# First layer's experts in order of load, 128 slots for six and 64 for ten, plain float32 products on unsplit weights

## The chip, the cores and the metric

The kernel runs on one core of a Trainium2 chip. The metric is the device time of one execution in microseconds (us), the median of several runs. All numbers here are of that core.

## The reference, cut to what matters

The reference is a two-layer hybrid diffusion backbone on 512 tokens (256 of a context, 256 of the image) of width 1024. Each layer has token mixers and then a mixture of 16 experts, of which each token takes two. Layer 0 computes its experts for all 512 tokens, layer 1 for the last 256. What the change touches is this:

```python
def _moe(h, router_w, router_b, w_gate, w_up, w_down):
    scores = jax.nn.sigmoid(h.astype(F32) @ router_w.astype(F32))
    ...
    _, idx = lax.top_k(jnp.where(in_grp, sel, -jnp.inf), TOP_K)
    ...
    combine = jnp.sum(jax.nn.one_hot(idx, N_EXPERTS, dtype=F32) * w[..., None], axis=1)
    out = jnp.zeros(h.shape, F32)
    for e in range(N_EXPERTS):
        act = jax.nn.silu(h @ w_gate[e]) * (h @ w_up[e])
        out = out + combine[:, e:e + 1] * (act @ w_down[e])
    return out.astype(h.dtype)
```

An expert's gate and up weights are 1024 x 512 each, its down weights 512 x 1024, all float32: six chunks of 1 MB.

## The kernel before, in words

A scheduler orders each engine's instructions when the kernel is built: tiles come from pools with a fixed number of buffers under a tag (`TILES`, `BANKS`), and the program's text sets priorities. Weights come through a ring of six 1 MB tiles, three under each of two tags (`RINGS`, `load`, L2064), in the order of use, issued on SP's queue.

Layer 0 (`moe`, L1780). `route` (L1600) scores the tokens on TensorE and VectorE (DVE), finds each token's two experts and its rank among an expert's tokens, by a running count on TensorE (L1659 to L1661, into `ps_route`), and the largest count, `rt_mxi`. `token_rows` (L1696) turns the normalised tokens to rows and keeps each as a high and a low part of type float32r (float32 words that TensorE multiplies at reduced precision). `gather` (L1809 on) builds a 0/1 selection `sel` of tokens against 128 slots for two experts at once (L1811), and multiplies it with the high and the low rows apart: 64 products of 256 columns (L1820) for a pair of experts. Copies to `xe` follow on DVE (L1826) and ScalarE (ACT, L1824).

Each expert then has 128 slots. Its weights are split into a high part by ACT (L152) and a low part by DVE (L153), 1024 columns at a time, and each product is made of three float32r products of 512 columns (L1804 to L1806): high x high, high x low, low x high. That makes 48 for gate and up and 24 for down. Between them stand the activation (L1862, L1863), the transposes of the activations (L1869, `ps_actT`) and their split (L1871, L1872). The result `y` of experts 0 to 14 is written to DRAM (L1894, on ACT's queue). Behind expert 14, GpSimd (POOL) fetches two rows of it for every token by eight indirect DMAs (L1904); ACT and DVE weight and add them (L1906, L1907). Expert 15 goes back to the tokens by products (L1914), and products with the identity (L1918) add the fetched rows in PSUM; DVE adds the result to the residual (`xT`, L1925). Three pieces of layer 1's conditioning (`between`, L1301, weights `in_w_ada`) run beside this end.

`overflow` (L1714) stands behind the first gather: each engine loads `rt_mxi` (L1734) and branches (L1735) around a loop over all experts that runs only where an expert has more tokens than slots.

Layer 1 (`moe_small`, L1929) already has 64 slots and plain float32 products on the weights as they come. The gate and up products of 256 columns run on the two 64-column halves of the array at a time (L1996), so do the down products of 512 (L2026). Its loads are the same ring.

## Time and profile before

| | |
|---|---|
| median of 3 runs | 1566.8 us (1566.14 to 1569.63) |
| profiled execution | 1576.39 us |
| its span, first to last instruction | 1574.6 us |
| mean granted TensorE clock | 0.929 |
| PE, DVE, ACT, POOL busy | 88%, 60%, 38%, 24% |
| DMA moved | 337.68 MB, 214 GB/s over the span |
| layer 0's experts, first product to the last y in DRAM | 533 to 861 us |
| its end, to the last residual | 861 to 900 us |
| layer 1's experts | 1312 to 1558 us |

PE is TensorE multiplying, PEld TensorE loading the operand that stays in the array, SP the engine that issues the loads of weights; PEq, SPq and so on are the engines' sequencers. A granted clock of 1.00 is TensorE's upper level, 2.4 GHz. A stretch is read by its own row, since stages of the program have different limits. Busy times of the profile are sums of instructions' durations; TensorE's instructions overlap, so what a run of products costs is read from the distance of their starts.

### The profile page before, as it was taken

To read this page: it belongs to the slowest core of one execution; us is meant where nothing else is said; L and a number is where in the kernel's file an instruction comes from. 1 tells how busy PE (TensorE), PEld (TensorE's weight loads), DVE (VectorE), ACT (ScalarE), POOL (GpSimd) and SP (SyncE) were. 2 spreads that over 40 slices of the span, in tenths; PEclk is the share of its full clock that TensorE was granted. 3 is DMA by queue.
4 is the path that set the end of the run, shared out by engine and by line. 5 is a ranking of instruction groups with operands and counts; after the bars stand their busy time and mean duration, and the time that the engine had idled before them with its cause. 6 is when DMAs were issued, how large, how long until landed. Compare 5 with 4: busy or idle time off the path is not lost. (4 is left out here: it accounts for less than half of the span.)

```text
span 1574.6 us, 28837 instructions
## 1 busy us (share of the span) xinstructions
PE 1390.1 (88%) x11950; PEld 1077.8 (68%) x11950; DVE 949.7 (60%) x1534; ACT 605.4 (38%) x908; POOL 372.1 (24%) x425
## 2 busy tenths in 40 slices
PE   5697869998998799999999877895999987999996
PEld 1596559888774688888887567675877765554553
DVE  5795793558444787879798669588345653111112
ACT  3353213433423576767677343421334350000001
POOL 1645252336101000000000665534133410000000
PEclk9797888999999899999999989796879998999999
DMA  9231334133426586969798712053325735999995
GB/s 380 68 99 46 96 138 136 63 108 122 176 80 263 199 338 268 366 269 368 267 383 334 311 32 98 30 171 130 122 80 198 274 133 212 389 393 401 405 418 214
DMA packets 83730, 337.68 MB, mean 214 GB/s; under 512 B 32278, under 2 KB 37208, under 8 KB 48904
## 3 DMA queue, kind: packets, MB, share of 16 engines
q1 hardware_dynamic: 79784, 320.36, 53.9%
q10 hardware_dynamic: 2160, 7.87, 1.2%
q0 software_dynamic: 1648, 7.54, 1.2%
q8 instruction: 97, 1.59, 0.4%
q14 instruction: 41, 0.34, 0.1%
HBM read 312.95 MB, written 22.77 MB: 213 GB/s over the span
## 5 line engine op out<-in xcount | busy, mean ns | idle before, releaser
L153 DVE TENSOR_TENSOR w_lo<-ring,w_hi 128x1024 fp32r<-128x1024 f32 x192 | 226.4, 1219 | 24.6 <-ACT w_hi L152 22.7
L152 ACT ACTIVATE w_hi<-ring 128x1024 fp32r<-128x1024 f32 x192 | 198.3, 1059 | 53.5 <-PE ps_up L1805 31.7
L1380 PE MATMUL ps_project<-h_hi,wi_lo 128*128 128x256 f32 (+1 forms) x568 | 138.3, 309 | 26.2 <-DVE wi_lo L153 26.1
L1380 PE MATMUL ps_project<-h_hi,wi_hi 128*128 128x256 f32 (+1 forms) x568 | 136.7, 308 | 13.8 <-ACT h_hi L1368 8.3
L1380 PE MATMUL ps_project<-h_lo,wi_hi 128*128 128x256 f32 (+1 forms) x568 | 134.1, 302 | 5.2 <-DVE h_lo L1369 5.2
L1996 PE MATMUL ps_up<-ring,xe 128*64 128x256 f32 x1024 | 120.8, 382 | 7.4 <-DMA ring<-in_w_moe 5.2
L1380 PEld LDWEIGHTS ps_project<-h_hi,wi_lo 128*128 128x128 f32 (+1 forms) x568 | 98.2, 203 | 34.5 <-DVE wi_lo L153 29.4
L1380 PEld LDWEIGHTS ps_project<-h_hi,wi_hi 128*128 128x128 f32 (+1 forms) x568 | 97.9, 203 | 18.7 <-ACT h_hi L1368 8.4
L1996 PEld LDWEIGHTS ps_up<-ring,xe 128*64 128x64 f32 x1024 | 72.0, 137 | 53.1 <-issue 14.9
L1805 PE MATMUL ps_up<-w_lo,xe 128*128 128x512 f32 x256 | 101.6, 397 | 4.9 <-DVE w_lo L153 4.3
L1380 PEld LDWEIGHTS ps_project<-h_lo,wi_hi 128*128 128x128 f32 (+1 forms) x568 | 97.5, 201 | 8.6 <-DVE h_lo L1369 5.7
L1804 PE MATMUL ps_up<-w_hi,xe 128*128 128x512 f32 x256 | 100.2, 394 | 1.9 <-PEq L1735 1.9
L1806 PE MATMUL ps_up<-w_hi,xe 128*128 128x512 f32 x256 | 100.0, 391 | 0.0
L2064 POOL DMA_DIRECT2D ring<-in_w_in x4 | 2.4, 609 | 384.7 <-PE ps_mods L1301 376.4
L153 DVE TENSOR_TENSOR wi_lo<-ring,wi_hi 128x1024 fp32r<-128x1024 f32 (+1 forms) x50 | 69.5, 1396 | 28.3 <-ACT wi_hi L152 20.8
L152 ACT ACTIVATE wi_hi<-ring 128x1024 fp32r<-128x1024 f32 (+1 forms) x50 | 51.2, 1032 | 88.4 <-DMA ring<-in_w_in 43.9
L2008 ACT ACTIVATE act<-ps_up 128x256 f32<-128x256 f32 x16 | 6.1, 383 | 160.4 <-PE ps_up L1996 133.2
L2029 DVE COPY y<-ps_down 128x512 f32<-128x512 f32 x16 | 11.1, 692 | 88.4 <-PE ps_down L2026 88.4
L2026 PE MATMUL ps_down<-ring,actT 128*64 128x512 f32 x256 | 58.6, 596 | 4.5 <-ACT actT L2017 4.5
L1805 PEld LDWEIGHTS ps_up<-w_lo,xe 128*128 128x128 f32 x256 | 48.1, 188 | 17.7 <-DVE w_lo L153 9.0
L1804 PEld LDWEIGHTS ps_up<-w_hi,xe 128*128 128x128 f32 x256 | 48.1, 188 | 12.0 <-ACT xe L1824 2.1
L1806 PEld LDWEIGHTS ps_up<-w_hi,xe 128*128 128x128 f32 x256 | 48.1, 188 | 9.1
(559 smaller groups left out, 3279.8 us busy)
## 6 DMA issues: line engine op xcount, KB each, us to landing
ring<-in_w_moe SPq DMA_DIRECT2D x192, 1024.0 KB
ring<-in_w_ada SPq DMA_DIRECT2D x46, 1024.0 KB
ring<-in_w_in SPq DMA_DIRECT2D x21, 1024.0 KB
ring<-in_w_out SPq DMA_DIRECT2D x8, 1024.0 KB
Y<-y ACTq DMA_DIRECT2D x15, 512.0 KB
xT<-in_xT SPq DMA_DIRECT2D x8, 512.0 KB
ring<-in_w_in POOLq DMA_DIRECT2D x3, 1024.0 KB
w_ada<-in_w_ada SPq DMA_DIRECT2D x4, 512.0 KB
```

The lines of the kernel that those rows point to most:

```text
L152: self.nc.scalar.activation(out[0], src, AF.Copy)
L153: self.nc.vector.tensor_tensor(out[1], src, out[0].bitcast(F32), ALU.subtract)
L1380: nc.tensor.matmul(p[:, c], x[a], w[b][:, c], start=i + a + b + o == 0, stop=i == n - 1 and a == 1, skip_group_check=True)
L1804: nc.tensor.matmul(p, xh, wh, start=first and i == 0, stop=False)
L1805: nc.tensor.matmul(p, xh, wl, start=False, stop=False)
L1806: nc.tensor.matmul(p, xl, wh, start=False, stop=last and i == n - 1)
L1996: nc.tensor.matmul(p[64 * c:64 * c + 64, 128 * j:128 * j + 256], x[4 * half + i], w[:, 512 * i + 256 * c:512 * i + 256 * c + 256], start=h ...
L2008: nc.scalar.activation(act, pu[:, :256], AF.Silu)
L2026: nc.tensor.matmul(p[64 * half:64 * half + 64], aT[:, f * 128 + 64 * c:f * 128 + 64 * c + 64], ds[half][:, 512 * i:512 * i + 512], start=i ...
L2029: nc.vector.tensor_copy(y, p)
L2064: queue.dma_start(w[:, :n], src)
```

## The change

Layer 0 gets a class `Experts` that layer 1 (now `moe_last`) uses as well. `route` with `by_load` sorts the experts on DVE: the counts are ranked by comparing each with each (L1695 to L1697), expert 0 always first; `rt_order` says which expert stands at which place, `rby` holds the ranks by place, and each place gets its first row in Y. The first six places (`BIG`) have 128 slots, the other ten 64; `rt_mxi` is now the largest number of tokens over a place's slots, and `overflow` runs if it is above zero. Places are taken in the order 0, 6, 1, 7, 8, 2, 9, 10, 3, 11, 12, 4, 13, 14, 5, 15, so that two small ones stand between big ones.

The gather adds high and low rows into one float32 `xe`: for place 0 alone 64 products of 128 columns, then five times 64 of 256 columns for a big and two small places. Nothing is split any more. A big place has 16 plain float32 products of 512 columns for gate and up and 8 for down; a small one has 32 of 256 columns and 8 of 512, two at a time on the halves of the array. The loads of all places but the first take the expert's number from a register of SP, which is read from `rt_order` (L1961). A small place's `y` has two writes to Y. The last place goes back to the tokens by eight plain float32 products. Layer 1's arithmetic stays as it was; its `route` leaves out what it did not use.

```diff
-CAPS = (128, 64)
+BIG, CAP_BIG, CAP = 6, 128, 64
...
+ROWS = CAP * VIA + (CAP_BIG - CAP) * BIG
+GROUPS = [(0,)] + [(BIG + 2 * i, i + 1, BIG + 2 * i + 1) for i in range(BIG - 1)]
...
+    v.scalar_tensor_tensor(key, cnt, 16.0, C["first16"], op0=ALU.mult, op1=ALU.add)
+    v.tensor_tensor(sq, key[:, None].to_broadcast([128, 16, 16]), key[:, :, None].to_broadcast([128, 16, 16]), ALU.is_gt)
+    v.tensor_reduce(place, sq, op=ALU.add, axis=AX.X)
...
+    v.tensor_copy(order, key)
+    v.tensor_tensor(big, rsel[:, :, None].to_broadcast([128, nt, 16, 16]), perm[:, None].to_broadcast([128, nt, 16, 16]),
+                    ALU.mult)
+    v.tensor_reduce(rby, big, op=ALU.add, axis=AX.X)
...
-    with k.tc.If(n > cap):
+    with k.tc.If(n > 0):
...
+                for j, rows in enumerate(hi + lo):
+                    nc.tensor.matmul(p[:, i * n:(i + 1) * n], rows[:, ms], sel[j % nt], start=j == 0, stop=j == 2 * nt - 1)
...
+                    if cap == 64:
+                        for c in range(2):
+                            nc.tensor.matmul(out[j][64 * c:64 * c + 64], x(4 * half + i),
+                                             w[:, 512 * i + 256 * c:512 * i + 256 * c + 256], **kw)
+                    else:
+                        nc.tensor.matmul(out[j], x(4 * half + i), w[:, 512 * i:512 * i + 512], **kw)
...
-        qs = [k.parts(w[:, 1024 * i:1024 * i + 1024], "w") for i in range(2)]
...
-            nc.tensor.matmul(p, xh, wh, start=first and i == 0, stop=False)
-            nc.tensor.matmul(p, xh, wl, start=False, stop=False)
-            nc.tensor.matmul(p, xl, wh, start=False, stop=last and i == n - 1)
...
+    first = [load(I["w_moe"][0, i], which=i % 2) for i in range(6)]
+    todo = gather(GROUPS[0])
+    overflow(k, I, h2, xT, mod, cwo, mxi, nt, 0)
+    _, at = nc.values_load_multi_w_load_instructions(order[:1, 1:], engines=(mybir.EngineType.SP,), min_val=0, max_val=15)
+    def weight(r, i):
+        if not r:
+            return first[i]
+        return load(I["w_moe"][bass.ds(at[r - 1], 1), i].rearrange("a p n -> p (a n)"), which=i % 2)
...
+        r, cap, _, sel = todo.pop(0)
+        aT = X.between(*pu, cap)
+        if len(todo) < 2 and groups:
+            todo += gather(groups.pop(0))
+        ds = [weight(r, 4 + half) for half in range(2)]
+        if todo:
+            pu = X.inward(todo[0][2], todo[0][1], lambda i: weight(todo[0][0], i))
+        y = X.outward(aT, cap, ds)
```

The order of the instructions moves at three places.

On PE, the end of the first gather and what follows. Before (`rt_mxi` and the branch behind it are the overflow test):

```order
L1820 MATMUL ps_gather<-sel,h_lo 128x256 x4
L1820 MATMUL ps_gather<-sel,h_hi 128x256 x4
L1820 MATMUL ps_gather<-sel,h_lo 128x256 x4
L1734 TENSOR_LOAD rt_mxi
L1735 COMPARE_AND_BRANCH
L1741 COMPARE_AND_BRANCH
```

The same place with the change:

```order
L1840 MATMUL ps_gather<-sel,h_hi 128x128 x4
L1840 MATMUL ps_gather<-sel,h_lo 128x128 x4
L1866 MATMUL ps_up<-ring,xe 128x512 x16
L1777 TENSOR_LOAD rt_mxi
L1778 COMPARE_AND_BRANCH
L1784 COMPARE_AND_BRANCH
```

The gather has half the columns, and the first expert's 16 gate and up products now stand ahead of the branch. Further on, PE's order for a round of one big and two small places, with the change, is this (128x512 down rows are the big place's, 64x512 the small ones'):

```order
L1863 MATMUL ps_up<-ring,xe 64x256 x16
L1901 MATMUL ps_down<-ring,actT 128x512 x8
L1863 MATMUL ps_up<-ring,xe 64x256 x8
L1878 MATMUL ps_actT<-consts_75,act 128x128 x2
L1863 MATMUL ps_up<-ring,xe 64x256 x16
L1894 MATMUL ps_down<-ring,actT 64x512 x5
L1863 MATMUL ps_up<-ring,xe 64x256 x8
L1894 MATMUL ps_down<-ring,actT 64x512 x3
```

Down products of one place lie between the up products of the next.

On SP, the loads behind the overflow loop. Before, the end of the loop and what follows:

```order
L1741 REGISTER_ALU
L1741 COMPARE_AND_BRANCH
L1741 UNCONDITIONAL_BRANCH
L1735 UNCONDITIONAL_BRANCH x2
L2064 DMA ring<-in_w_moe 128x2048 x90
L2064 DMA ring<-in_w_ada 128x2048 x6
```

With the change, ahead of the branch:

```order
L2090 DMA ring<-in_w_ada 128x2048 x10
L2090 DMA ring<-in_w_moe 128x2048 x6
L1961 TENSOR_LOAD rt_order
L1961 ISA x28
L1777 TENSOR_LOAD rt_mxi
L1777 ISA x2
L1961 ISA x2
L1778 COMPARE_AND_BRANCH
```

and behind the loop:

```order
L1784 UNCONDITIONAL_BRANCH
L1778 UNCONDITIONAL_BRANCH x2
L2090 ISA
L2090 DMA ring<-in_w_moe 128x2048
L2090 ISA
L2090 DMA ring<-in_w_moe 128x2048
```

The order's registers are filled ahead of the branch (ISA rows are register operations), and each load behind it has one register operation of its own.

On DVE, behind the running count in `ps_route`. Before:

```order
L1662 TENSOR_TENSOR rt_rsel<-rt,ps_route 128x64
L1665 TENSOR_REDUCE rt_mx<-ps_route 128x1
L1667 TENSOR_SCALAR rt<-ps_route 128x64
L1811 TENSOR_TENSOR sel<-consts_76,rt_rsel 128x1024
L1666 CAST rt_mxi<-rt_mx 128x1
```

With the change:

```order
L1668 TENSOR_TENSOR rt<-rt,ps_route 128x64
L1695 SCALAR_TENSOR_TENSOR rt_l<-ps_route,consts_76 128x16
L1675 TENSOR_TENSOR rt<-rt 128x64
L1696 TENSOR_TENSOR rt_big<-rt_l 128x256
L1927 TENSOR_TENSOR sel<-consts_76,rt 128x512
L1676 TENSOR_REDUCE rt_s<-rt 128x4
L1697 TENSOR_REDUCE rt_l<-rt_big 128x16
L1675 TENSOR_TENSOR rt<-rt 128x64
L1698 TENSOR_TENSOR rt_l<-rt_l,consts_76 128x256
```

The first selection stands one place later and has half the columns; most of the sort stands behind it, 21 rows of `route` ahead of the first copy of `xe` on DVE and 22 more ahead of the second.

## Rows read from the trace of the kernel before

**Rows 1.** Busy time of an engine: us, share of the span, instructions.

```profile
PE 1390.1 (88%) x11950; PEld 1077.8 (68%) x11950; DVE 949.7 (60%) x1534; ACT 605.4 (38%) x908; POOL 372.1 (24%) x425
```

**Rows 2.** Stretches: length, busy us and count by engine, granted clock, DMA share, GB/s.

```profile
522.00:533.35 11.35, 9.35 (x65) 9.17 (x65) 7.16 (x33) 4.64 (x7) 0.00 (x0) 0.85 0.01 4
533.35:860.50 327.15, 320.91 (x1632) 269.63 (x1633) 275.32 (x273) 234.26 (x267) 0.00 (x0) 1.00 0.84 323
860.50:899.70 39.20, 33.59 (x200) 23.71 (x198) 22.79 (x32) 12.97 (x15) 21.94 (x16) 0.96 0.78 309
...
1311.70:1558.35 246.65, 229.85 (x1689) 132.22 (x1688) 36.11 (x76) 18.90 (x41) 0.00 (x0) 1.00 0.95 384
1350.00:1550.00 200.00, 188.47 (x1378) 106.07 (x1376) 29.46 (x60) 12.24 (x30) 0.00 (x0) 1.00 1.00 403
1390.40:1400.10 9.70, 8.42 (x69) 4.92 (x63) 2.21 (x5) 0.38 (x1) 0.00 (x0) 1.00 1.02 421
```

**Rows 3.** Timeline of PE, fp32r products of an expert: start, us, what.

```profile
542.16 0.39 PE L1806 MATMUL ps_up<-w_hi,xe 128*128 128x512 f32 x1
...
543.07 0.39 PE L1804 MATMUL ps_up<-w_hi,xe 128*128 128x512 f32 x1
```

**Rows 4.** Costliest groups: busy us, mean ns, idle time before and its releaser.

```profile
L153 DVE TENSOR_TENSOR w_lo<-ring,w_hi 128x1024 fp32r<-128x1024 f32 x192 | 226.4, 1219 | 24.6 <-ACT w_hi L152 22.7
```

**Rows 5.** Timeline of PE, first gather, branch and first product.

```profile
522.13 1.23 PE L1820 MATMUL ps_gather<-sel,h_hi 128*128 128x256 f32 x4 [1.66 <-DVE rt_mxi L1666]
...
525.56 0.64 PE L1820 MATMUL ps_gather<-sel,h_hi 128*128 128x256 f32 x4
...
530.83 0.64 PE L1820 MATMUL ps_gather<-sel,h_lo 128*128 128x256 f32 x4
533.35 0.47 PE L1804 MATMUL ps_up<-w_hi,xe 128*128 128x512 f32 x1 [1.88 <-PEq L1735]
```

**Rows 6.** Chain that ended last, layer 1's experts: start, us, what.

```profile
1372.94 3.43 PE ps_down L2026 x16
1376.37 3.45 PE ps_up L1996 x32
...
1390.45 9.61 DMA ring<-in_w_moe
...
1408.04 0.38 PE ps_actT L2015 x2
...
1475.73 5.98 DMA ring<-in_w_moe
```

**Rows 7.** Group, line and timeline of plain float32 products and transposes.

```profile
L2026 PE MATMUL ps_down<-ring,actT 128*64 128x512 f32 x256 | 58.6, 596 | 4.5 <-ACT actT L2017 4.5
L1326 PE MATMUL ps_rstd<-rs,consts x10: 379/592/697, 17.5 to 1565.9; 128*128 128x512 f32 x6, 128*128 128x256 f32 x4
608.38 0.49 PE L1869 MATMUL ps_actT<-consts,act 128*128 128x128 f32 x3
896.35 2.05 PE L1918 MATMUL ps_last<-consts,ya 128*128 128x128 f32 x16 [0.29 <-DVE ya L1907]
```

**Rows 8.** Timeline of DVE, `route` and the first gather.

```profile
520.50 0.22 DVE L1662 TENSOR_TENSOR rt_rsel<-rt,ps_route 128x64 f32<-128x64 f32 x1 [2.41 <-PE ps_route L1661]
520.86 1.22 DVE L1811 TENSOR_TENSOR sel<-consts,rt_rsel 128x1024 fp32r<-128x1024 f32 x1
524.24 0.69 DVE L1826 CAST xe<-ps_gather 128x512 fp32r<-128x512 f32 x1 [0.43 <-PE ps_gather L1820]
```

**Rows 9.** Lines L1734, L2064 on SP's sequencer: ns least/median/most, first and last start.

```profile
L1734 SPq FUSED_REGOPS  x2: 175/181/187, 522.7 to 1307.8; - x2
L2064 SPq DMA_DIRECT2D ring<-in_w_moe x192: 327/328/1358, 490.1 to 1544.1; - x192
```

**Rows 10.** DMA queue of the loads, 1350 to 1550 us: packets, MB, share of 16 engines.

```profile
q1 hardware_dynamic: 11046, 80.46, 99.3%
```

**Rows 11.** Timeline of DVE and POOL behind the 15th expert; indirect DMAs, us to landing.

```profile
859.87 0.69 DVE L1888 COPY y<-ps_down 128x512 f32<-128x512 f32 x1 [0.17 <-PE ps_down L1806]
869.17 1.03 POOL L1904 DMA_INDIRECT ya<-Y,rt_slot  x1 [0.93 <-issue]
877.99 1.16 POOL L1904 DMA_INDIRECT yb<-Y,rt_slot  x1 [0.30 <-issue]
yb<-Y,rt_slot POOLq DMA_INDIRECT x4, 8.9
```

More of the change, by code (lines that the diff above doesn't have):

```diff
@@ L1711, in token_rows, with overflow @@
     return hi, lo
-def overflow(k, I, h2, xT, mod, cwo, mxi, nt, cap, layer):
+def overflow(k, I, h2, xT, mod, cwo, mxi, nt, layer):
     nc, C = k.nc, k.C
@@ L1841, in gather @@
-        return out
-    def into(xs, e, j):
-        p = k.bank("up", "p")[:cap]
-        for half in range(2):
-            product(p, xs[4 * half:4 * half + 4], split(weight(e, j + half)), half == 0, half == 1)
-        return p
-    def weight(e, i):
-        return load_e(e, i) if e else first[i]
-    Y = S["Y"][layer]
-    back, before, ys = [], [], []
-    xs, after = gather(0)
-    first = [load_e(0, i) for i in range(6)]
-    overflow(k, I, h2, xT, mod, cwo, mxi, nt, cap, layer)
-    pg = into(xs, 0, 0)
@@ new lines, in outward @@
+    def outward(self, aT, cap, ds):
+        k, nc = self.k, self.nc
+        y = k.u("y", 8 * cap)
+        if cap == 64:
+            p = k.bank("down", self.acts[2])
+            for i in range(4):
+                for half in range(2):
+                    nc.tensor.matmul(p[64 * half:64 * half + 64], aT[i], ds[half][:, 512 * i:512 * i + 512], start=i == 0,
+                                     stop=i == 3)
+            nc.vector.tensor_copy(y, p)
+        else:
+            for half in range(2):
+                p = k.bank("down", self.acts[2])
+                for i in range(4):
+                    nc.tensor.matmul(p, aT[i], ds[half][:, 512 * i:512 * i + 512], start=i == 0, stop=i == 3)
+                o = y[:, 512 * half:512 * half + 512]
+                if half:
+                    nc.vector.tensor_copy(o, p)
+                else:
+                    nc.scalar.activation(o, p, AF.Copy)
+        return y
@@ L1908, in moe @@
                 before.append(ya)
-    ps = [k.bank("last", "aaaabbpp"[m])[:, :nt * 128] for m in range(8)]
-    for m, p in enumerate(ps):
-        for i in range(16 - VIA):
-            for n, (u, w) in enumerate(((0, 0), (0, 1), (1, 0))):
-                nc.tensor.matmul(p, ys[i][u][:, m * 128:(m + 1) * 128], back[i][:, w], start=i == 0 and n == 0, stop=False,
-                                 skip_group_check=True)
+    ps = [k.bank("last", "aaaabbpp"[m]) for m in range(8)]
+    for m in range(4):
+        for half in range(2):
+            hs = slice(64 * half, 64 * half + 64)
+            nc.tensor.matmul(ps[4 * half + m], y[hs, m * 128:(m + 1) * 128], back[hs], start=True, stop=False,
+                             skip_group_check=True)
     for t in range(nt):
@@ L1982, in moe_small @@
-    xs, sel = gather(0)
+        sel = k.u("sel", nt * 4 * CAP).bitcast(F32R).rearrange("p (t g s) -> p t g s", t=nt, g=4)
+        selection(k, sel, rsel[:, :, e:e + 4], CAP)
+        x = X.gather([sel[:, t].rearrange("p g s -> p (g s)") for t in range(nt)], 4 * CAP, hi, lo)
+        return [(lambda i, a=g * CAP: x(i, a, a + CAP), sel[:, :, g]) for g in range(4)]
+    todo = gather(0)
     first = [load_e(0, i) for i in range(6)]
-    overflow(k, I, h2, xT, mod, cwo, mxi, nt, cap, layer)
+    overflow(k, I, h2, xT, mod, cwo, mxi, nt, 1)
@@ L2030, in moe_small @@
+        _, sel = todo.pop(0)
+        aT = X.between(*pu, CAP)
+        b = X.back(sel, cw[:, :, e])
+        if len(todo) == 2 and e < 12:
+            todo += gather(e + 3)
+        ds = [weight(e, 4 + half) for half in range(2)]
+        if todo:
+            pu = X.inward(todo[0][0], CAP, lambda i: weight(e + 1, i))
+        y = X.outward(aT, CAP, ds)
         for m in range(4):
@@ L2034, in moe_small @@
                                  skip_group_check=True)
-        if e % 4 == 3:
-            xs, sel = after, asel
     k.exp_ln()
```

343 lines of the change are left out of this document (157 added, 186 removed).

## The prediction

> **What bounds the kernel now.** I read the busy shares first: PE is busy 88% of the span [rows 1], so time comes mostly out of TensorE's work. Then the table of stretches [rows 2]. The one that the change rewrites, 533.35 to 860.50 us, has PE busy 320.91 of 327.15 us at granted clock 1.00, the 2.4 GHz level, with DMA at 0.84: TensorE bounds it, and its idle time is 6.2 us. The second layer's expert stretch shows what comes next if TensorE gets less to do: there DMA stands at 0.95 to 1.00 and moves 403 GB/s. The order of work says who waits for whom in between; the timeline and the chain give prices.
>
> The sum is made against the profiled execution (1576.39 us, span 1574.6, so 1.8 us outside). It is 9.6 us above the median 1566.8; I take the difference as a constant and apply the gain to the median. A change of under 0.2% (3 us) could not be told from none.
>
> **What is removed.** Layer 0 makes 72 fp32r products of 512 columns an expert, one each 0.227 us (four steps from 542.16 to 543.07 [rows 3]), 16.3 us an expert. The splits behind them, 192 of 1.22 us on DVE [rows 4] and as many on ACT, go too; they lie beside PE's work, which waited little for them, so I count nothing for them but the 6.2 us that I leave in place as idle time. Seven later gathers of 64 matmuls go; five remain.
>
> **What stands there now,** from the start of the first gather at 522.13 us [rows 5] to the last down product of the 15th expert, after which DVE copies y at 859.87 [rows 11]; all after that hangs on this y.
>
> 1. Plain float32. The trace shows each such product as two records: 256 records for layer 1's 128 down products [rows 7]. Of those, 16 records (8 products, two at a time on the halves of the array) take 3.43 us [rows 6]: 0.86 us for a 512-column pair. A full-width product is a record of the same 592 ns at its median (L1326 [rows 7]), up to 697; I take 0.86 us, the upper end 0.86 x 697/592 = 1.01. A big expert has 24: 20.6 us, six make 124. (Per big expert that is dearer than the 16.3 us now; the gain comes from the small ones.)
> 2. A small expert: 32 records of up products take 3.45 us [rows 6], half of an expert's, so 6.9 us, and its down products 3.43. In the row of 15 experts there are nine small, and by the order a quarter of the 16th's up products stands ahead: 9.25 x 6.9 = 64 and 9 x 3.43 = 31.
> 3. Five gathers of 256 columns: sixteen groups of four at 0.479 us (eleven steps from 525.56 to 530.83 [rows 5]) are 7.7 us each: 38.
> 4. First gather, 64 fp32r matmuls of 128 columns, a shape that the trace lacks. Below: half of the 256-column one, 0.06 us, 3.8 in all. Above: a plain float32 one of 128 columns, 2.05/8 = 0.256 us (L1918 [rows 7]), 16.4 in all. Nearest is the row of the same shape, at clock 0.96; I take 0.2 us, 13.
> 5. Transposes: three in 0.49 us for big ones, two in 0.38 [rows 6, 7]: 6 x 0.65 + 9 x 0.38 = 7. The branch: 1.9 us idle as now [rows 5].
>
> These make 279 us. To them come:
>
> 6. Idle time between groups as now: 6.2.
> 7. The sort. DVE gets some 20 small operations, four of 256 columns (0.2 to 1.2 us each) and two of 1024 (1.22) ahead of the copies of x [rows 8]: about 8 us, beside a first gather of 13. The selection for expert 0 is ahead of nearly all of it, and is half as large as now. The second copy of x may come late: 0 to 5 us, I take 2. Order and register values reach SP by one load and 28 register operations of 0.18 us [rows 9], 5.5 us, done before the first ring slot is free; each later load costs 0.18 on top of 0.33, well within 2.6.
> 8. The ring. 80.46 MB in 200 us [rows 10] is 2.61 us a 1 MB load. Two small experts in a row need 12 loads (31 us) in about 21 us of PE; six lie in the ring. The first slot is free 1.7 us after the first small one starts. The shortest wait for a load in the chain is 5.98 us [rows 6], at most 3.4 more than its 2.61; so the fourth load behind that slot lands by 1.7 + 3.4 + 10.4 = 15.5, just when it is needed, and the last by 20.8, needed at 17.2 or later: 0 to 3.5 us in each of five rounds, 0 to 17 in all. I take 5, since by the order the next expert's up products mostly stand ahead of the last two loads' down products. A whole round has 20.6 + 2 x 10.3 + 7.7 + 1.4 = 50 us of PE against 18 loads, 47 us.
>
> Sum 292 us, so the copy of y starts at 814.3 in place of 859.87: **45.6 us sooner**. The tail from there [rows 2, 11] (Y to DRAM, eight indirect gathers with 8.9 us to landing, weighting, identity products, xT until 900) follows y and POOL, not PE's products; the last expert's own work gets shorter beside it. I leave its 39 us, give or take 4. Layer 1 computes the same with fewer route operations behind DVE's other work: nothing; its expert stretch hangs on 96 loads [rows 2]. The mixers between, 412 us, are re-sequenced by the scheduler: I allow 2% of that, 8 us, each way. 1566.8 - 45.6 gives **1521 us**.
>
> **Rivals.**
>
> *Register-addressed loads are served slower (ends slower).* Place: SP's loads from the seventh on. About 86 loads stand between the first free slot (538.6) and the 15th y, with 5.8 MB of Y writes (14 us) and a last down of 7: y at 559.6 + 86 c. At c = 2.61 that is 784, 30 us ahead of PE; from 2.96 loads set the time, from 3.49 the kernel is slower. The only transfers here with computed addresses are the indirect ones: eight of 512 KB from 869.17 to 877.99 + 8.9 [rows 11], 4.4 us a megabyte; by that y comes at 938 and the time is 1645. Against: other loads shared that stretch, which moved 309 GB/s in all [rows 2], and a load remains 128 rows of 8 KB. Chance 0.06.
>
> *The ring becomes the bound, gain smaller.* Down weights hold two of six slots until the next expert's up products are through. The chain of layer 1 has a wait of 9.61 us right behind down products [rows 6]; yet PE was busy 8.42 of those 9.7 us [rows 2], and in the whole stretch it idled 16.8 us for 16 experts. If uneven slots make a load cost 3.2 us, y comes at 835: 1541. Chance 0.13.
>
> *The clock falls at those waits.* The first gather shows the price: its first four groups took 522.13 to 525.56, 3.4 us, against 1.9 later, at mean clock 0.85 in that stretch [rows 2, 5]: 1.5 us. One such fall for each of 15 experts costs 23 us: 1544. Against: that same 9.7 us window had granted clock 1.00, and so had all 200 us around it [rows 2]. The Trainium skill (TensorE: Matmul & The Clock Gate, HAM oscillation) says that a kernel whose matmul groups wait for DMA in between loses its clock at each wait. By that rule it would be this 1544; the trace disagrees for layer 1, where other matmuls fill the wait. Chance 0.06.
>
> *More is gained:* first gather at its lower bound (9 less), no ring wait, no late x: 16 us more, 1505. Chance 0.10.
>
> *It doesn't do what it says:* the overflow loop runs because a seventh expert exceeds 64 slots, at least 96 more loads of 2.61, 250 us: 1772 or more. The loads worked out from the reference's inputs are 65 for expert 0, then 117, 104, 92, 81, 64, and 60 at most for the other ten, so no place overflows. Chance 0.01.
>
> **How the numbers follow.** The forecast has 0.64; its own terms span 1505 to 1535. The range 1498 to 1546 takes in the smaller gains and the larger one with 8 us of mixers, and leaves out the two slow rivals and the tail of the second. Faster by over 0.2%: 0.91, from the forecast, the larger gain and nearly all of the two smaller ones; within 0.2%: 0.02; slower: 0.07.
>
> **What would show it.** In the profile after: the copy of the 15th y at 810 to 820; big products 0.86 us apart and eight half-width downs in 3.43; first gather 10 to 16 us; DMA at 0.9 or more from 540 on with clock 1.00; PE's waits for the ring under 12 us; tail 35 to 43 us. I am wrong if PE's idle time in the stretch passes 35 us with loads over 3 us apart (second rival, or the first), if full-width products are 1 us apart, or if the mixers moved by more than 8.

## The result, and the profile after

The changed kernel takes 1555.7 us at the median of 20 runs (1546.0 to 1567.3); the kernel before, on the same chip, 1566.3 us. The ratio is 0.9926, with a 95% interval of 0.9903 to 0.9949: faster, by about 11 us where 46 were forecast. The time lies outside the range of 1498 to 1546.

The profiled execution took 1553.63 us, 2 us under its median, where that of before [rows 2] lay 10 above its own. So the stretches below differ by 22 us in all, and the medians by 11. Table of stretches of the profile after (length; busy us and count of PE, PEld, DVE, ACT, POOL; granted clock; DMA share; GB/s): the first gather, from there to the last write of a result to Y, the tail to the last residual, the mixers, layer 1's experts:

```profile
517.71:531.42 13.71, 13.71 (x65) 13.71 (x65) 9.34 (x45) 0.39 (x1) 0.00 (x0) 0.50 0.01 2
531.42:831.77 300.35, 286.96 (x1395) 150.82 (x1397) 30.86 (x50) 24.81 (x48) 0.00 (x0) 0.98 0.85 331
831.77:881.03 49.26, 41.09 (x232) 22.67 (x228) 22.08 (x38) 13.66 (x16) 22.37 (x17) 0.90 0.88 353
881.03:1278.99 397.96, 336.08 (x3556) 275.32 (x3557) 261.67 (x461) 144.87 (x268) 160.33 (x194) 0.89 0.38 127
1278.99:1551.86 272.87, 244.05 (x1746) 140.22 (x1746) 45.82 (x102) 23.26 (x49) 0.00 (x0) 0.98 0.87 351
```

The profile of before, cut at the same events, with the first two rows as one:

```profile
522.13:860.65 338.52, 330.40 (x1697) 278.91 (x1698) 282.50 (x304) 239.05 (x273) 0.00 (x0) 1.00 0.81 313
860.65:903.24 42.59, 36.68 (x215) 24.93 (x214) 26.18 (x40) 15.36 (x18) 25.12 (x17) 0.96 0.79 313
...
1307.32:1574.63 267.31, 239.22 (x1746) 138.84 (x1746) 46.92 (x117) 23.07 (x49) 0.00 (x0) 0.99 0.89 358
```

From the first gather to the last write, 338.5 us became 314.1: 24 less, about half of the forecast. The tail grew from 42.6 to 49.3, and layer 1, whose arithmetic is the same (1746 records of products in both), from 267.3 to 272.9. Minus 24, plus 7, plus 6 make minus 12, near the 11 us of the medians. The other 10 us between the profiles lie ahead of the first gather (4) and in the mixers (6: 404.1 became 398.0). Both stretches have the same products in the two kernels, and both differ about as much between two executions of one kernel: the change's first gather starts at 517.7 and, run again, at 521.0, and the mixers of before take 404.1 and 398.4. So no part of the change's gain is shown to lie there.

**Inside the experts.** The first and the only small place with its down products in one piece, and the round that follows (timeline of PE: start, us, what; two records are one plain float32 product):

```profile
576.38 3.65 PE L1894 MATMUL ps_down<-ring,actT 128*64 128x512 f32 x16
579.96 10.57 PE L1866 MATMUL ps_up<-ring,xe 128*128 128x512 f32 x24
...
619.34 2.74 PE L1894 MATMUL ps_down<-ring,actT 128*64 128x512 f32 x10
621.83 1.97 PE L1863 MATMUL ps_up<-ring,xe 128*64 128x256 f32 x16
623.61 1.88 PE L1894 MATMUL ps_down<-ring,actT 128*64 128x512 f32 x6
626.60 0.44 PE L1878 MATMUL ps_actT<-consts,act 128*128 128x128 f32 x2 [1.11 <-DVE act L1875]
627.83 2.79 PE L1894 MATMUL ps_down<-ring,actT 128*64 128x512 f32 x10 [0.80 <-ACT actT L1880]
630.55 3.70 PE L1866 MATMUL ps_up<-ring,xe 128*128 128x512 f32 x8
```

Eight whole products take 3.58 us, to the next start. The eight that are split into five and three take 2.49 and 1.88 of PE's time: 4.37. Five products, two pairs and a single one, take about three slots of 0.86, so the single one has a slot to itself. Then PE waits. DVE at that moment:

```profile
625.52 0.69 DVE L1896 COPY y<-ps_down 128x512 f32<-128x512 f32 x1 [11.40 <-PE ps_down L1894]
626.13 0.41 DVE L1875 TENSOR_TENSOR act<-act,ps_up 128x256 f32<-128x256 f32 x1
```

In DVE's order the copy of the last result stands ahead of the next place's activation. It waits for the last down product, so the activation, whose operand from ACT was there at 624.25, waits as well, and PE's transposes behind it. PE's waits from 515 to 881 us (line, releaser: us in total, times, longest):

```profile
PE ps_actT L1878 <- DVE act L1875: 6.0, 5, 1.5
PE ps_down L1894 <- ACT actT L1880: 3.7, 5, 0.8
...
PE ps_up L1863 <- DMA ring<-in_w_moe: 2.3, 4, 1.1
```

The activations make PE wait longer than the ring does (3.8 us with its two smaller rows).

**The tail.** The copy of the 15th result, the first fetch on POOL, and the fetches' median time to landing (to set against [rows 11]):

```profile
831.01 0.69 DVE L1904 COPY y<-ps_down 128x512 f32<-128x512 f32 x1 [9.77 <-PE ps_down L1901]
842.93 1.15 POOL L1998 DMA_INDIRECT ya<-Y,rt_slot  x1 [352.82 <-DMA ring<-in_w_ada]
yb<-Y,rt_slot POOLq DMA_INDIRECT x4, 14.9
```

From the copy to the first fetch it is 11.9 us where it was 9.3, and a fetch lands after 14.9 where it was 8.9. SP issues most of the last loads of `w_ada` in between, since the ring comes free late (start, us, what):

```profile
832.89 4.80 SPq L2090 DMA_DIRECT2D ring<-in_w_ada  x4
```

### The profile page after: what moved, and what is told of

Its sections match the earlier page's. It is cut to its first block, busy times and chain, and to the rows that moved or that the text cites. A ratio compares the mean times of both kernels' runs of the same rounds, so it can differ in the third digit from the quotient of the medians.

```text
span 1551.9 us, 27894 instructions
## 1 busy us (share of the span) xinstructions
PE 1358.3 (88%) x11730; PEld 952.4 (61%) x11730; DVE 701.8 (45%) x1310; ACT 391.5 (25%) x683; POOL 372.1 (24%) x425
## 5 line engine op out<-in xcount | busy, mean ns | idle before, releaser
L1863 PE MATMUL ps_up<-ring,xe 128*64 128x256 f32 x1664 | 201.5, 387 | 11.6 <-DMA ring<-in_w_moe 9.3
L1863 PEld LDWEIGHTS ps_up<-ring,xe 128*64 128x64 f32 x1664 | 118.5, 138 | 91.7 <-issue 26.8
L1894 PE MATMUL ps_down<-ring,actT 128*64 128x512 f32 x416 | 107.5, 613 | 5.8 <-ACT actT L1880 4.7
L1866 PE MATMUL ps_up<-ring,xe 128*128 128x512 f32 x192 | 86.8, 607 | 0.5 <-DMA ring<-in_w_moe 0.5
L155 DVE TENSOR_TENSOR wi_lo<-ring,wi_hi 128x1024 fp32r<-128x1024 f32 (+1 forms) x50 | 72.8, 1463 | 18.3 <-ACT wi_hi L154 15.8
L1894 PEld LDWEIGHTS ps_down<-ring,actT 128*64 128x64 f32 x416 | 31.4, 139 | 61.6 <-issue 51.1
L1866 PEld LDWEIGHTS ps_up<-ring,xe 128*128 128x128 f32 x192 | 36.3, 194 | 50.4 <-issue 49.7
L1305 PE MATMUL ps_mods<-ring,sc 128*32 128x512 f32 x368 | 56.0, 660 | 1.2 <-DMA ring<-in_w_ada 0.7
L1840 PE MATMUL ps_gather<-sel,h_hi 128*128 128x256 f32 (+1 forms) x256 | 49.4, 309 | 6.5 <-DVE sel L1927 4.6
L1840 PE MATMUL ps_gather<-sel,h_lo 128*128 128x256 f32 (+1 forms) x256 | 47.9, 303 | 0.0
L1840 PEld LDWEIGHTS ps_gather<-sel,h_hi 128*128 128x128 f32 x256 | 40.4, 213 | 11.4 <-issue 5.0
```

What stands on the lines that cost most here:

```text
L155: self.nc.vector.tensor_tensor(out[1], src, out[0].bitcast(F32), ALU.subtract)
L1305: nc.tensor.matmul(p[32 * j:32 * j + 32], sc[:, 4 * r + j], w[r][j], start=r == 0, stop=r == 1)
L1840: nc.tensor.matmul(p[:, i * n:(i + 1) * n], rows[:, ms], sel[j % nt], start=j == 0, stop=j == 2 * nt - 1)
L1863: nc.tensor.matmul(out[j][64 * c:64 * c + 64], x(4 * half + i), w[:, 512 * i + 256 * c:512 * i + 256 * c + 256], **kw)
L1866: nc.tensor.matmul(out[j], x(4 * half + i), w[:, 512 * i:512 * i + 512], **kw)
L1894: nc.tensor.matmul(p[64 * half:64 * half + 64], aT[i], ds[half][:, 512 * i:512 * i + 512], start=i == 0, stop=i == 3)
```

## The experiments

Each ratio stands against the kernel before, run beside it. The stretches are cut as above, in us, each from one profiled execution, which can lie 10 us from its kernel's median:

| kernel | first gather to last write | tail | mixers | layer 1 | median | ratio (95%) |
|---|---|---|---|---|---|---|
| before | 338.5 | 42.6 | 404.1 | 267.3 | 1566.3 | |
| before again (r2) | 338.6 | 42.6 | 398.4 | 268.1 | 1571.6 (one run) | |
| the change | 314.1 | 49.3 | 398.0 | 272.9 | 1555.7 | 0.9926 (0.9903 to 0.9949) |
| the change again (r1) | 315.5 | 47.9 | 394.5 | 275.3 | 1556.8 | 0.9936 (0.9916 to 0.9956) |
| e1 | 312.2 | 47.9 | 399.4 | 286.0 | 1572.4 | 1.0024 (0.9995 to 1.0052) |
| e2 | 315.1 | 35.8 | 401.9 | 290.9 | 1563.0 | 0.9956 (0.9928 to 0.9985) |
| e3 | 311.1 | 46.9 | 394.0 | 290.8 | 1561.4 | 0.9960 (0.9929 to 0.9991) |
| e4 | 310.6 | 47.7 | 419.4 | 272.3 | 1578.2 | 1.0052 (1.0020 to 1.0083) |
| b1 | 347.1 | 34.8 | 395.7 | 270.1 | 1574.6 | 1.0055 (1.0029 to 1.0081) |
| e5 | 328.3 | 43.9 | 393.1 | 286.4 | 1574.5 | 1.0039 (1.0015 to 1.0063) |
| e6 | 314.5 | 43.4 | 396.9 | 283.8 | 1564.3 | 0.9984 (0.9960 to 1.0009) |
| e7 | 301.8 | 46.3 | 394.3 | 279.8 | 1549.7 | 0.9908 (0.9888 to 0.9927) |
| e8 | 301.9 | 46.5 | 395.2 | 290.0 | 1552.3 | 0.9920 (0.9895 to 0.9945) |
| e10 | 301.5 | 38.5 | 454.8 | 273.8 | 1592.1 | 1.0164 (1.0121 to 1.0208) |
| e11 | 300.5 | 41.4 | 390.4 | 271.1 | 1528.4 | 0.9757 (0.9727 to 0.9788) |

### e1: small down products in one piece

```diff
-        y = X.outward(aT, cap, ds)
+        with k.tc.high_priority():
+            y = X.outward(aT, cap, ds)
```

> Edit: the down products get the scheduler's highest priority, so the eight of a small place stay together and no product is left alone on one half of the array; nothing else of the arithmetic moves. Theory A (broken pairs: in the changed kernel small down products are issued five, then others, then three, so that two of the eight run alone, about 0.9 us lost for each of nine small places, plus about 1 us of waiting behind them): the down products of a small place go from 5.3 us to about 3.5, and the 15th y comes 8 to 16 us sooner than at 831 (313 us behind the first gather), kernel 5 to 15 us faster than the changed one, about 1543 to 1550. Rival B (the ring is the bound): y stays within 3 us, and PE's waits for the ring grow from 3 us to over 10. Rival C (the loss is elsewhere, in clock or in gather): pairs mend, the stretch shortens by under 4 us.

The down products came whole: PE's time on the nine small places' downs went from 48.1 to 32.6 us (start to start). But the stretch lost only 2 us of it. PE's waits, and below SP's, from 515 to 845 us:

```profile
PE ps_actT L1878 <- DVE act L1875: 10.0, 10, 1.5
PE ps_up L1863 <- DMA ring<-in_w_moe: 8.4, 7, 3.0
...
SPq L2091 <- PE ps_down L1901: 75.5, 11, 12.5
```

With nothing behind the last up product to fill in, the waits for the activation rose from 6.0 to 10.0 and those for the ring from 2.3 to 8.4, since a slot with down weights is held until they are used. And the scheduler gave layer 1 another order, 286 us where it had 273. So the pieces had filled part of these waits, and mending them alone wins next to nothing in this stretch.

### e2 and b1: w_ada's part ahead of the experts

```diff
-PARTS = ((3, 6, 3), (8, 0, 0))
+PARTS = ((3, 9, 0), (8, 0, 0))
```

e2 does it to the change, b1 to the kernel before.

> Edit: the three pieces of layer 1's conditioning that ran beside the end of layer 0's experts (six loads of 1 MB and their products) run ahead of the experts, beside the output projection. Theory A (in the changed kernel these loads share the DMA engines with the eight fetches of rows of Y, which land after 14.9 us in place of 8.9): landing falls to 9 to 10 us and the stretch from the 15th y to the last residual from 50 us to 38 to 43; total 6 to 12 us faster than the changed kernel if the loads find room ahead (DMA at 0.53 there), nothing if they push the first gather back by as much. Rival B (the end is long for another reason: DVE beside POOL, 16 late adds): landing falls and the end stays at 47 us or more. Rival C: landing does not change.

> Edit: the kernel before, with the three pieces of conditioning moved ahead of the experts as in the run of that kind on the changed kernel. Theory (before the change these loads were through by the time of the fetches, so there is nothing to gain): landing stays at 8.9 us, the end of layer 0 from the 15th y at 38 to 43 us, total within 5 us of the kernel before. Rival (the move helps either kernel, so it is no part of the change's loss): the end shortens by 6 us or more here too.

With the loads of `w_ada` out of the tail it takes 35.8 us in e2 (the change 49.3) and 34.8 in b1 (before 42.6). The fetches in e2:

```profile
yb<-Y,rt_slot POOLq DMA_INDIRECT x4, 7.3
```

That is half of 14.9: the loads are what held the fetches. I had expected nothing from b1, and its rival came true: in the kernel before, too, these loads cost the tail 8 us (13 in the change). Without them the two kernels' tails are 1 us apart, so the change's longer tail is these loads'. Neither median fell: b1 pays 8.6 us where the part now stands, and e2's layer 1 takes 18 us more than the change's, again in an order that the edit does not speak of.

The products of `mods` now stand around the first gather, and show its price at the other level of the clock. Two groups of four in the change, and then in e2:

```profile
518.62 1.05 PE L1840 MATMUL ps_gather<-sel,h_lo 128*128 128x128 f32 x4
519.47 1.05 PE L1840 MATMUL ps_gather<-sel,h_hi 128*128 128x128 f32 x4
```

```profile
517.92 0.61 PE L1840 MATMUL ps_gather<-sel,h_lo 128*128 128x128 f32 x4
518.37 0.61 PE L1840 MATMUL ps_gather<-sel,h_hi 128*128 128x128 f32 x4
```

From start to start a group takes 0.85 us in the change, at granted clock 0.50 (1.2 GHz) from its first product to its last, and 0.45 in e2, whose stretch has 1.00. The forecast's 13 us were right in size, by a wrong reason: the shape costs 7.2 us, and the clock the rest.

### e3: the first gather with 256 columns

```diff
-        n = sum(CAP_BIG if r < BIG else CAP for r in group)
+        n = sum(CAP_BIG if r < BIG else CAP for r in group) if group[0] else 2 * CAP_BIG
```

> Edit: the first gather takes a second expert's selection along, which is not used: 64 products of 256 columns in place of 128, and its selection on DVE is twice as large (1.2 us for 0.7). Theory A (the 128-column products leave TensorE's clock at 0.50 for the whole first gather, 13.7 us, and for part of the first expert's up products): with 256 columns the clock rises as in the kernel before, the gather takes 9 to 10 us, the up products behind it 14 for 15.5; 15th y 4 to 6 us sooner, kernel 3 to 6 us faster. Rival B (a product of this type under 256 columns costs as much as one of 256 at any clock, and the clock is low for another reason): the gather stays near 13.7 us at clock 0.50, total unchanged.

With twice the columns the gather takes less time, 10.4 us at granted clock 0.71 in place of 13.7 at 0.50: the clock rises inside it. The experts' stretch behind it has clock 1.00 throughout, and from the gather to the last write it is 3 us less. Layer 1's order took that back.

### e4: the loads' addresses as constants

```diff
-    _, at = nc.values_load_multi_w_load_instructions(order[:1, 1:], engines=(mybir.EngineType.SP,), min_val=0, max_val=15)
+    at = (6, 5, 7, 1, 12, 9, 10, 11, 2, 13, 4, 15, 3, 14, 8)
...
-        return load(I["w_moe"][bass.ds(at[r - 1], 1), i].rearrange("a p n -> p (a n)"), which=i % 2)
+        return load(I["w_moe"][at[r - 1], i], which=i % 2)
```

> Edit: the loads of the places take the expert's number from a list written into the program, which is the order that these inputs give; the sort stays. No register load, no register operation in front of a load. Theory A (addresses from registers cost nothing in the transfer; SP waits for free slots anyway): loads land at the same pace; the DMA rate in full stretches stays at about 2.6 us a load; what changes comes from the scheduler's other order of PE, which keeps most small down products together: y 0 to 14 us sooner for that alone, as in the run with the down products first. Rival B (register-addressed loads are the loss): loads per us go up by over 5%, PE's waits vanish, y 15 us sooner or more and more than in the run with the down products first.

The experts' stretch moves its bytes at the same rate as with registers, 331 GB/s (second row of the stretches above):

```profile
533.45:830.31 296.86, 281.55 (x1379) 148.82 (x1381) 31.14 (x50) 24.74 (x48) 0.00 (x0) 0.98 0.84 332
```

It is 3.5 us shorter, but its order on PE is another too, and its small down products take 43.8 us where the change's take 48.1; so no cost of the registers is shown. The median is worse since the scheduler set the mixers differently, 419 us.

### r1 and r2: the change and the kernel before again

> The changed kernel once more, beside the others of this call, for its stages in a second profile. If the two profiles of it agree (first gather to 15th y 313 us, y to the last residual 50, residual to layer 1's first gather 398, layer 1's experts 251), the stage differences between kernels are the program's; if they differ by over 5 us in a stage, that stage varies by execution and differences of that size are not read.

> The kernel before once more, one look, for its stages in a second profile. The first one's execution was 10 us above the median. If that is the mixers between the two expert layers (404 us there, clock at its lower level for 105 us, where other kernels' profiles have 393 to 402 and 87 to 96), this profile shows 393 to 398 there and the same experts as before: first gather to last residual 381 us, layer 1 from its first gather to the end 267. If it is another stage, the comparison of stages changes by as much.

Layer 0's stretches repeat within 1.4 us, layer 1's within 2.5, the mixers' within 6. So a difference of 13 us and more in layer 1 is hardly one of the execution.

### e5 and e6: PE in the text's order, then the loads in the order of use

e5 holds every product and transpose of the experts in program order; e6 also takes the next place's up weights ahead of this one's down weights, as PE uses them:

```diff
-                            nc.tensor.matmul(out[j][64 * c:64 * c + 64], x(4 * half + i),
+                            self.mm(out[j][64 * c:64 * c + 64], x(4 * half + i),
...
-        ds = [weight(r, 4 + half) for half in range(2)]
         if todo:
             pu = X.inward(todo[0][2], todo[0][1], lambda i: weight(todo[0][0], i))
+        ds = [weight(r, 4 + half) for half in range(2)]
```

> Edit: in both layers' experts every product on TensorE is pinned behind the one written before it, so the order is up products of the next place, down products of this one, transposes, and so on, with no pieces; loads are issued in the order written, this place's down weights ahead of the next one's up weights. Theory A (pieces are the loss in both layers): the small down products cost 3.5 us each, layer 0 from first gather to 15th y 295 to 303 us, layer 1's experts 245 to 252; total 8 to 20 us faster than the changed kernel. Rival B (the ring: down weights lie in two of six slots while the up products behind them wait for loads): PE waits over 15 us for loads in layer 0, stretch 308 us or more, small down products mended all the same.

> Edit: as the run with TensorE in the order of the text, and in addition the next place's up weights are loaded ahead of this place's down weights, which is the order in which they are used, so slots come free in the order in which loads need them. If the ring is what is left (rival B of that run): PE's waits for loads in layer 0 fall under 6 us and the stretch from first gather to 15th y to 288 to 298 us, layer 1's experts to 245 to 250, total 12 to 25 us faster than the changed kernel. If loads are simply too many for the DMA engines, the waits stay as they are.

PE's waits from 515 to 845 us, in e5 and then in e6:

```profile
PE ps_up L1831 <- DMA ring<-in_w_moe: 15.8, 13, 2.6
```

```profile
PE ps_actT L1834 <- DVE act L1881: 13.0, 10, 1.5
...
PE ps_down L1831 <- DMA ring<-in_w_moe: 1.6, 3, 1.2
```

Whole products with the loads out of step make the ring the wait (15.8 us, the stretch 14 us longer than the change's). With the loads in PE's order the ring's waits are gone, and what is left is the activation, 13 us in ten waits. The stretch is no shorter than the change's (314.5 where I expected 288 to 298), and the median is 8 us above that of the change run beside it (1556.8).

### e7 and e8: the result's copy behind the next activation

e7 is e6 with the copy of a result taken behind the next place's activation on DVE, in both layers, and e2's part. e8 is e7 with layer 1's text as in the change, its order left to the scheduler.

```diff
-        nc.vector.tensor_tensor(act, act, pu, ALU.mult)
+        self.k.tc.keep_in_program_order(nc.vector.tensor_tensor(act, act, pu, ALU.mult))
+        if then:
+            then()
...
+        then = lambda r=r, cap=cap, y=y, copy=copy: write(r, cap, y, copy)
```

> Edit: the run with TensorE in the order of the text and loads by use, and in addition each place's result is copied from PSUM behind the next place's activation on DVE (so the transposes do not wait for a copy that waits for down products), and the three pieces of conditioning run ahead of the experts. Theory (what was lost is down products in pieces, the waits of 1.1 to 1.5 us behind them, two to four falls of the clock of 3.4 us, and the collision at the end): PE's waits for the activation in layer 0 fall from 13 us to under 3 and for loads stay under 5; first gather to 15th y 285 to 298 us, first gather to last residual 322 to 336 (363 in the changed kernel), layer 1 from its first gather to the end 262 to 272; total 20 to 40 us faster than the changed kernel. Rival (the DMA engines are the bound of layer 0 by now): waits for loads of 15 us or more take the place of the others and the stretch stays above 305.

> Edit: layer 0 as in the run before this one of the call, layer 1 exactly as in the changed kernel, its order left to the scheduler, which here breaks its down products into 5 and 3, 6 and 1 and 1, 7 and 1, as in the runs with down products first, mods ahead and first gather of 256. Theory (the order that the scheduler happens to give an untouched layer moves the time): layer 1 from its first gather to the end takes 284 to 292 us against 262 to 272 with the order pinned, and the whole is 12 to 25 us slower than that run; layer 0 the same within 4 us. Rival (layer 1's length follows from something that differs between executions): both are within 6 us.

PE's waits in e7 from 515 to 845 us:

```profile
PE ps_back L1834 <- DVE back L1923: 23.2, 1, 23.2
PE ps_gather L1831 <- DVE sel L1936: 6.8, 6, 1.4
PE ps_actT L1834 <- DVE act L1881: 1.5, 1, 1.5
PE ps_down L1831 <- DMA ring<-in_w_moe: 1.4, 2, 1.1
```

The waits for activation and ring are gone together; those for the gathers' selections have grown from 2.1 us in the change to 6.8. The stretch is 301.8 us, 12 under the change, though 4 us of `mods` products now lie in it; 2.6 of the 12 come ahead of the first transposes, where e2's part has raised the clock. That misses my 285 to 298, and the median of 1549.7 is no 20 us below the change. The tail of 46.3 is far from e2's 35.8, by an error of mine that the first line shows. The copy of the last small result now stood behind the weighted adds, which wait for the fetches:

```profile
841.82 1.28 DVE L2001 SCALAR_TENSOR_TENSOR ya<-yb,rt_wm,ya 128x1024 f32<-128x1024 f32 x1 [1.19 <-DMA yb<-Y,rt_slot]
843.02 0.68 DVE L1905 COPY y<-ps_down 128x512 f32<-128x512 f32 x1
```

e8 has the same layer 0 (301.9) and 290.0 us in layer 1, 10 more than e7, as its one profile shows. The medians are only 2.6 us apart, not the 12 to 25 that I expected: e7's profiled execution lies 10 us under its median, e8's 6 above. What an order in layer 1 is worth is read better from all runs. PE's order there, by tiles and shapes, is one and the same in e1, e2, e3 and e8, with down products in pieces of down to half a product, and takes 286.0 to 290.9 us. In the change, r1 and e10 it is another, with whole down products, and takes 272.9 to 275.3; in e4 and e11, nearly that one, 272.3 and 271.1. PE's waits for the ring in layer 1, in the change and then in e2:

```profile
PE ps_up L1863 <- DMA ring<-in_w_moe: 7.1, 8, 2.1
```

```profile
PE ps_up L1863 <- DMA ring<-in_w_moe: 19.1, 11, 2.9
```

So most of those 13 to 18 us are waits for loads, which that order of the products brings with it.

### e10 and e11: the tail mended, and GpSimd's loads

e10 is e8 with the fetches' priority raised, the weighted adds behind the last result's copy on DVE, and GpSimd's weight loads held in program order; layer 1's text is e8's, and yet its down products come out whole. (Its expectation calls e7 the seventh run; that of e11 calls e10 the twelfth.) e11 takes out that hold and nothing else:

```diff
-            d = queue.dma_start(w[:, :n], src)
-            if queue is nc.gpsimd:
-                tc.keep_in_program_order(d)
+            queue.dma_start(w[:, :n], src)
```

> The first layer of the seventh run (whole small downs, the 15th result behind the next activation, w_ada's part taken ahead), with the end of that layer mended: the 15th result's copy on DVE goes ahead of the weighted adds again, and the fetches of result rows are issued ahead of GpSimd's late loads; layer 1 is left to the scheduler. Theory (the loss against the forecast was the small places' broken pairs and the waits behind them, plus a tail lengthened by w_ada's loads, plus whatever order the scheduler gives layer 1): the stretch from the first gather to the last result's write stays at 300 to 304 us, the tail from there to the last residual falls from 46 to 34 to 40, layer 1 from its first gather to the end is 268 to 276, the median 20 to 35 us below the kernel before, ratio 0.978 to 0.986. Rival (the row fetches are held by something other than w_ada's loads and the order on DVE and GpSimd): the tail stays at 44 or more, and the ratio at 0.988 to 0.992. Rival (layer 1's order is worth more than the tail): layer 1 is 284 or more and the median no lower than 1550 against 1566.

> The twelfth run's kernel with one thing taken out: GpSimd's weight loads are no longer held in program order, so the mixers between the layers get the order that the seventh run had. Theory (the 60 us that the twelfth run lost in the mixers came from that hold, and the gain of layer 0 is kept once the mixers stand as in the other runs): first gather to last residual 338 to 344 us, mixers 392 to 402, layer 1 270 to 276, the median 25 to 38 us below the kernel before, ratio 0.976 to 0.984. Rival (what layer 0 ends earlier the mixers give back whatever their order, by loads that are not there yet or by the clock): mixers 415 or more, ratio above 0.99.

In e10 both parts of layer 0 came as expected (301.5 and 38.5), layer 1 too (273.8), and the kernel is 26 us slower than before: the mixers took 454.8 us. POOL issues there, in the midst of its own work on the mixers, four loads, at 897.67 to 1023.42, of which e11 issues three ahead of the fetches, by 829.14 (the first, timeline of POOL in e10):

```profile
897.67 0.60 POOL L2207 DMA_DIRECT2D ring<-in_w_in  x1
```

Without the hold (stretches of e11 behind the first gather, which takes 11.5):

```profile
531.91:820.88 288.97, 278.69 (x1444) 153.79 (x1446) 31.98 (x53) 25.66 (x49) 0.72 (x1) 1.00 0.89 356
820.88:862.30 41.42, 24.64 (x118) 16.35 (x119) 29.10 (x33) 11.53 (x11) 23.02 (x16) 0.75 0.61 234
862.30:1252.72 390.42, 331.57 (x3557) 273.71 (x3555) 259.11 (x462) 143.75 (x268) 160.24 (x193) 0.88 0.37 130
```

1528.4 us, 38 below the kernel before and 27 below the change; layer 0 from the first gather to the last residual takes 341.9 us where it took 381.1. The rival, that the mixers take back whatever layer 0 gives, has fallen: they take 390.4. Part of it is luck: e11's layer 1 came out in an order near the change's (271.1 us), which no edit asked for. In e8, with a layer 0 only 6 us longer, it took 290.0, and e8's median is 24 us above e11's. The tail is 41.4 and not e10's 38.5, since POOL's third load waits for its slot ahead of the first fetch, which starts at 830.0 in place of 826.1. A round in e11 (timeline of PE):

```profile
653.62 7.13 PE L1831 MATMUL ps_up<-ring,xe 128*64 128x256 f32 x64
660.68 7.13 PE L1831 MATMUL ps_down<-ring,actT 128*128 128x512 f32 x16
667.65 0.38 PE L1834 MATMUL ps_actT<-consts,act 128*128 128x128 f32 x2
667.96 7.13 PE L1831 MATMUL ps_up<-ring,xe 128*64 128x256 f32 x64
```

A small place's up products in one piece, the big place's downs behind them, no wait at the transposes: what the forecast had summed.

## Why the prediction was wrong

The mechanism was right: the plain products' price, the places' sizes, the slots, TensorE as what bounds the stretch. The sum failed at its step 2 and at two things that it left as they were, the tail and layer 1. From the first gather to the copy of y it took 313.3 us (517.71 to 831.01) where 292 were forecast. Without their waits the products took 300 of them where 277 were forecast, and 12 of these 23 us are the small down products'. The times below run from start to start and contain the waits behind a product.

- **Step 2, small down products: 31 us forecast, 48.1 measured** over nine places, 42.9 without waits. I took a place's 3.43 us from layer 1's chain [rows 6], where the eight products stand together. The order that I had before me showed them as five and three, and I did not price it. Eight of nine places were broken; whole they cost 32.6 (e1). Of the 15.5 us between, 5.2 are waits right behind a piece, and a clock that falls in two pieces (4.42 us for ten records where others take 2.49 to 2.78) some 3.4; the rest, 7 us, is put down to single products with a slot of their own. Runs e1 to e7 show that this is one knot: where the downs stood whole, waits for the activation and the ring took the place of the pieces, and only with whole downs, loads in their order and the copy behind the activation did the stretch fall, to 301.8.
- **Step 1, the big places: 124 forecast, 131.9 measured**, of which 3.1 are waits. A product costs 0.88 us at best (24 records in 10.57). The first place's sixteen ups took 17.0 us, some 3 more than that price: the clock that the first gather left low was 0.57 in their first 3.6 us, and e2, with clock 1.00 there, has them in 14.1. In e11 all of the big places' products take 126.5.
- **Step 2, the ups:** 64 forecast, 68.9 measured; 32 records took 3.60 us where the forecast had 3.45. **Step 5, transposes:** 7 forecast, 12.2 measured, of which 5.0 are waits behind them, mostly for the copy of their result; without these it was right. **Step 3:** 38 against 39.3, right.
- **Step 4, the first gather: 13 against 13.7**, right in size; the mechanism was the clock (0.50), not the shape (7.2 us in e2).
- **Steps 6 to 8, idle time: 13.2 forecast and 13.4 found** (300.35 less 286.96, within the times above), right in sum and wrong in kind: 4 us for the ring, most of the rest for activations. That the sums agree is luck. DMA stood at 0.85 there, not at the 0.9 that I had named as the sign.
- **The tail: "follows y and POOL", 39 give or take 4; it took 50.0** from the copy of y to the last residual, where before had 43.4 by that count (the forecast's 39 end at 899.70; before's last adds to the residual run to 903.24). The error is a step that moves past a queue: SP's loads of `w_ada` came behind the experts' loads, into the fetches. e2 and b1 show it: without those loads the tails are 35.8 and 34.8.
- **Layer 1: "nothing"; it took 6 us more.** The products are the same, their order is not, and an order was worth 13 to 18 between the change and e1 to e3. Why the change's own layer 1 is slower than that of before, by 5 to 8 us over two profiles of each, was not settled; its ring waits are 7.1 and 7.2 us against 5.2 and 3.0, its clock 0.98 and 0.96 against 0.99 and 0.98.
- **The mixers** moved by at most 10 us, near the 8 allowed; e4 and e10 (419 and 455) show that the allowance holds only for an order of its kind.

Of the rivals, the register-addressed loads fell (e4: 332 GB/s against 331; from 741 to 746 us all DMA of the change moved 426, above the 403 of [rows 2]). That rival's 5.8 MB of Y are 5.5, 1,344 rows of 4 KB, which moves its times by under 1 us. The ring as the bound is not what happened in the change (under 4 us of waits), but stands close behind it: e1 and e5 made it the wait. The falling clock was partly real. The profile shows it after a broken place with a wait behind it:

```profile
741.17 0.44 PE L1878 MATMUL ps_actT<-consts,act 128*128 128x128 f32 x2 [1.11 <-DVE act L1875]
742.41 4.49 PE L1894 MATMUL ps_down<-ring,actT 128*64 128x512 f32 x10 [0.80 <-ACT actT L1880]
```

The window from 741 to 746 us has granted clock 0.67, one from 799 to 804 too; the same sequence at 626.60 kept 1.00. So it fell at two places, not at fifteen, and cost some 3 us, not 23. That count is one execution's: in e2's, four such pieces take 4.28 to 4.42 us, in windows of 5 us at clock 0.66, and in e3's none does (2.72 to 2.77, clock 1.00). What decides it was not tried. The Trainium skill (TensorE: Matmul & The Clock Gate, HAM oscillation) tells of such falls where groups of matmuls wait for DMA in between; the trace agrees that a wait can cost the clock, but here the waits were for an activation, and at two of the four such places it did not.

That most of the forecast's gain was there to be had is shown by e11: its 341.9 us for layer 0 are 39 under before, the tail included.

## What to carry to other kernels

Price a run of products by the order in which it will stand, not by the run of another stage: two products on the halves of the array pay only where they stand in pairs, and a scheduler can take pairs apart. Where a faster engine is the gain, mend three things together: the products' order, the order of the loads that free their slots, and the copies that stand ahead of the next activation on another engine; the first alone, and the first two together, gained no more than 2 us in this stretch (e1, e6). And read the untouched stages of the new program as well: their order came out anew with many of the edits, and cost up to 18 us in layer 1 and up to 60 in the mixers.

## What the runs showed of the hardware that I had not expected

A product on one half of the array without its partner takes the pair's time: five and three apart take 2.72 and 1.86 us to the next start (at 685.99 and 692.34), eight together 3.58. It lasts in e11, where the second half's weights come late for one place of most rounds (timeline of PE):

```profile
620.63 1.02 PE L1831 MATMUL ps_down<-ring,actT 128*64 128x512 f32 x2
622.41 3.65 PE L1831 MATMUL ps_down<-ring,actT 128*64 128x512 f32 x14 [0.76 <-DMA ring<-in_w_moe]
```

The first product goes alone, so the last does too, and such a place takes 4.7 to 5.4 us, waits of 0.1 to 0.8 among them, at four of nine places.

A gather with twice the columns was faster: 64 products of 256 columns took 10.4 us (e3) where 64 of 128 took 13.7. PEld is busy through the whole of both; the clock stayed at 1.2 GHz in the latter, while in e3 it rose within the gather. What in a stretch of products raises the clock was not tried further. At clock 1.00 the 128 columns took 7.2 us (e2) and the later gathers of 256 took 7.9, so half of the columns saved a tenth and not a half.

A row fetch of 512 KB lands after 5.2 to 7.5 us, by its median, in the runs that have no load of `w_ada` near the end (e2, b1, e7, e8, e10, e11), after 8.9 in the kernel before, and after 9.5 to 18.7 where these loads come late (the change, with 14.9, and e1, e3 to e6).
